# A transformer layer with pooling, neighbourhood attention and routed experts: five reorderings ahead of the main loop

## The chip, the cores and the metric

One core of a Trainium2 chip runs the whole layer. The metric is the device time of one execution in microseconds (us), from the first to the last instruction of the program and what lies around it. The engines are PE (TensorE, matmuls), DVE (VectorE), ACT (ScalarE), POOL (GpSimd) and SP (SyncE, whose queue issues most of the DMAs).

## What is computed

The reference, cut to one layer and one batch of 512 tokens with 1,024 columns and 256 context tokens:

```python
mod = silu(c) @ ada_w + ada_b          # six columns of 1,024: shift1, scale1, gate1, shift2, scale2, gate2
hx = modulate(rmsnorm(x, g1n), sh1, sc1);  hc = the same of ctx
zx = hx @ w_in                         # 512 columns each: pool, q, k, v;  context: k, v
pool_x = multiscale_pool(zx_pool, pool_w) * pool_scale      # windows 2, 4, 8, 16
attn_x = neighbourhood_attention(q, k, v, k_ctx, v_ctx, rpb)
x = x + gate1 * (concat(pool_x, attn_x) @ w_out)
h2 = modulate(rmsnorm(x, g2n), sh2, sc2)
# experts: per token 8 heads, top 16 of 128 + 128 keys, top 16 of the sums -> 128 of 16,384 experts
x = x + gate2 * sum_k softmax(score)_k * gelu(h2 . u_k) * v_k
out = rmsnorm(x, final_g)
```

## The kernel before, in words

The work stands in one program of some 22,000 instructions, in stages.

**Start and `w_in`.** The tokens are turned and normalised, the first two modulation columns are made, and then eight groups of 256 columns of `w_in` are multiplied (loop of line 344), in the order 4, 5 (keys), 6, 7 (values), 2, 3 (queries), 0, 1 (pooling). Every product is made as three matmuls of a high and a low half of each operand (`mm3`, line 66); the halves of a weight block come from `load_split` (line 82): a 1 MB load into one of three `raw` buffers, a copy on ScalarE (`whi`, lines 72 and 550) and a subtraction on VectorE (`wlo`, lines 73 and 556), each with two buffers. `ada_more` (line 320) makes the later modulation columns: four 1 MB loads through the same three `raw` buffers and eight multiply-adds of 1,024 columns on VectorE (line 130). Columns 2, 3, 4 stand in this loop, column 5 (the second gate) in the attention.

**Attention.** 32 steps, four token blocks by eight heads (loop of line 511). `scores` (line 437) is two or three matmuls, one VectorE reduction (line 453) and an exponential on ScalarE; `turn` (line 458) transposes on TensorE; `values` (line 466) multiplies. A turn follows its score by two steps, values by one more. Into these steps `pooling` of the four groups is put (line 392: three to six VectorE adds, one matmul, then a copy and a subtraction into `mixh` and `mixl`), the last gate at step 17, and six of the sixteen units of the out-projection (`out_unit`, line 492: 24 matmuls for 128 tokens by 256 columns). The other ten come behind.

**Norm2.** `norm_T` (line 186) squares each of the four token tiles, makes a diagonal of the root, and for each of eight column blocks turns and scales the four tiles on TensorE (line 195), modulates on ScalarE (line 199), and splits on VectorE (lines 201 and 202). `keepD` turns one of the tiles back (line 572).

**Routing.** Eight blocks of query weights give 16 query products; `topk_unit` (line 632) scores one token tile on four keys sets and takes the top 16 on VectorE. `decode` (line 696) turns them into experts for three tiles, on VectorE. Then 24 batches build the dense weights W (`wbatch_dve`, `wbatch_pe`), which go to memory in twelve writes. Beside all of it run the first 52 of 128 products of the expert matrix `u` with the tokens (`ahead_unit`, line 644: 24 matmuls, a Gelu, every second one a write to memory and a split of the next pair). `pace` (line 844) puts them in: each decode part has a cost in us of VectorE, written out by hand (4.3, 2.9, 0.3, 6.5, 3.2, 4.2 for a tile), the cost divided by `UNIT_DVE` is added to a credit, each W batch adds `UNIT_W`, and a whole credit issues a product.

**Main loop.** For each of the 128 blocks of 128 experts: a product with `u` if it was not made ahead (line 982), a multiplication by W (line 1005), and 18 matmuls with `v` (line 1026). The fourth token tile goes another way, by 256 gathers on POOL with one VectorE operation each (lines 889 and 895).

**Order.** From the end of the first `w_in` group to the end of norm2 the framework orders each engine's instructions itself: by the order in the program as priority, by when it thinks operands and buffers are ready, and by its own durations. From `wq_unit` on, the order on each engine is the one written. Each engine runs its own queue in order; so does SyncE with the loads that it issues.

Of the kernel before, what the change touches and what calls it, by code (L numbers as in the profile page):

```python
# [16 lines left out]
P = 128  # L17
D = 1024
# [9 lines left out]
NAHEAD = 52  # L28
UNIT_DVE = 3.02
UNIT_W = 1.02  # L30
GF, GA = 2, 1
GX = 5
N5 = 17
# [19 lines left out]
def _build(tc, nc, es, A, out, taps):  # L53
# [131 lines left out]

    def norm_T(tiles, a_of, b_of, hi, lo, runs, pool, pst, keep=None):
        n = len(tiles)
        dg = pool.tile([P, 4, P], F32, tag="pr", name="dg", bufs=3)
        for t, x in enumerate(tiles):
            r = rstd_of(x, pool)  # L190
            nc.vector.tensor_scalar(dg[:, t, :], identf, r, None, op0=OP.mult)
        for k in range(KC):
            pt = pst.tile([P, 512], F32, tag="T", name="pT")
            for t in range(n):
                nc.tensor.matmul(pt[:, t * P:(t + 1) * P], tiles[t][:, k * P:(k + 1) * P], dg[:, t, :],
                                 start=True, stop=True)
            tmp = pool.tile([P, 512], F32, tag="pr", name="htmp", bufs=3)
            for dst, src in runs:
                act(dst(tmp), src(pt), AF.Identity, bias=b_of(k), scale=a_of(k))
            w = n * P  # L200
            nc.vector.tensor_copy(hi[:, k, :w], tmp[:, :w])
            nc.vector.tensor_sub(lo[:, k, :w], tmp[:, :w], hi[:, k, :w].bitcast(F32))
            if keep is not None:
                keep(k, tmp)
# [115 lines left out]
    def ada_more(c):  # L320
        acc = ada_dve(c, fp, "m8", 2)
# [16 lines left out]

    def order_kj(g):
        if g == 4:  # L340
            return [(k, j) for k in range(KC) for j in range(2)]
        return [(k, j) for j in range(2) for k in range(KC)]

    for g in (4, 5, 6, 7, 2, 3, 0, 1):
        whi, wlo = {4: w_first, 5: w_next}.get(g) or load_split(A["w_in"][g])
        if g in (3, 0, 1):
            ada_more({3: 2, 0: 3, 1: 4}[g])
        sec, half = divmod(g, 2)
        if sec == 3:
            for t in range(6):  # L350
                pt = psf.tile([P, 512], F32, tag="S", name="pz")
                sh, sl = (hhi, hlo) if t < 4 else (chi, clo)
                c0 = (t if t < 4 else t - 4) * P
                for k in range(KC):
                    mm3(pt[:, :256], sh[:, k, c0:c0 + P], sl[:, k, c0:c0 + P], whi[:, k, :], wlo[:, k, :],
                        k == 0, k == KC - 1)
                act(VN[t][:, half * 256:half * 256 + 256], pt[:, :256], AF.Copy)
            continue
        pzs = [psf.tile([P, 512], F32, tag="S", name="pz") for _ in range(2)]
        for k, j in order_kj(g):  # L360
            cs = slice(j * P, (j + 1) * P)
            mm3(pzs[j], whi[:, k, cs], wlo[:, k, cs], hhi[:, k, :], hlo[:, k, :], k == 0, k == KC - 1)
        if g == 4:
            start.close()
        for j in range(2):
            jj = half * 2 + j
            cs = slice(j * P, (j + 1) * P)
            pt = pzs[j]
            if sec == 2:
                act(KT[jj][:, :SEQ], pt, AF.Copy)  # L370
                pc = psf.tile([P, 512], F32, tag="O", name="pz2")
                for k in range(KC):
                    mm3(pc[:, :CTX], whi[:, k, cs], wlo[:, k, cs], chi[:, k, :], clo[:, k, :], k == 0, k == KC - 1)
                act(KT[jj][:, SEQ:], pc[:, :CTX], AF.Copy)
            elif sec == 1:
                for e in range(2):
                    r = slice(e * 64, e * 64 + 64)
                    act(QZ[jj][r, e, 0:384], pt[r, 64:448], AF.Copy, scale=-0.125)
                    act(QZ[jj][r, e, 384:512].rearrange("p (a c) -> p a c", c=64), edges(pt[r, :]), AF.Copy, scale=-0.125)
            else:  # L380
                xp = fp.tile([P, 528], F32, tag="xp", name="xp", bufs=4)
                nc.vector.memset(xp[:, 0:8], 0.0)
                nc.vector.memset(xp[:, 520:528], 0.0)
                act(xp[:, 8:520].rearrange("p (r c) -> p r c", c=64), pt.rearrange("p (c r) -> p r c", r=8), AF.Copy)
                xps.append(xp)

    mixh = persist.tile([P, KC, SEQ], F32R, tag="hhi", name="mixh")
    mixl = persist.tile([P, KC, SEQ], F32R, tag="hlo", name="mixl")

    def pooling(g, x):
# [44 lines left out]
    def scores(b, h):  # L437
# [18 lines left out]
        return b, h, pr, kb  # L456

# [112 lines left out]
    def keepD(k, tmp):  # L570
        pt = psf.tile([P, 512], F32, tag="O", name="pD")
# [3 lines left out]
    norm_T(xq, lambda k: a2[:, k:k + 1], lambda k: modT[:, 24 + k, 0:1], hhi, hlo,  # L575
           [(lambda t: t, lambda p: p)], fp, psf, keepD)
# [86 lines left out]
    for u in range(20):  # L663
# [586 lines left out]
```

## Time and profile before

| what | value |
|---|---|
| median of 3 runs | 1554.18 us (1554.18 to 1554.66) |
| profiled execution | 1554.02 us, its span 1552.2 us |
| PE busy | 1504.5 us, 97% of the span |
| DVE busy | 1208.3 us, 78% |
| ACT busy | 614.0 us, 40% |
| POOL busy | 348.7 us, 22% |
| mean granted clock of TensorE | 0.991 |
| DMA | 396.67 MB, mean 256 GB/s |

Busy time is the time in which an engine runs an instruction; matmuls are pipelined and their ends are modelled, so a TensorE busy all the time is not one at its peak. A granted clock of 1.00 stands for 2.4 GHz and 0.50 for 1.2 GHz; a mean between them over a stretch tells how much of it was at half.

### The profile page before, as it was taken

Reading aid. Unit: us, or ns where it says so; the run is one execution under the profiler, and the core shown is the slowest. Engines: PE = TensorE matmul, PEld = TensorE weight load, DVE = VectorE, ACT = ScalarE, POOL = GpSimd, SP = SyncE. Lnnn points to the kernel's source line nnn. Section 1 sums busy time; section 2 is a strip of 40 time slices with the busy share of each in tenths; the row PEclk is TensorE's granted clock in tenths of the full one; section 3 lists DMA queues with packets and bytes.
Section 4 is the critical chain, followed back from the end, with each engine's and each line's share of the span. In section 5 each row is a group of like instructions: output and inputs, shape, how many; then the busy total and the mean of one; then the engine's idle time right before and its main releaser. Section 6 shows DMA issues by size and latency. Waiting matters only on the chain.

```text
span 1552.2 us, 22062 instructions
## 1 busy us (share of the span) xinstructions
PE 1504.5 (97%) x8553; PEld 1348.8 (87%) x8553; DVE 1208.3 (78%) x2211; ACT 614.0 (40%) x884; POOL 348.7 (22%) x278
## 2 busy tenths in 40 slices
PE   7999999999989999998999999999999999999997
PEld 4897789888979999997889898889988988899886
DVE  6618853538989999867887888779788887887885
ACT  3522553423334455554333433333333333343343
POOL 0000000000000000000244444344444444445431
PEclk9999999999999999999999999999999999999999
DMA  9318610132235467687799999999899989898971
GB/s 363 132 55 305 241 55 1 55 119 92 99 117 183 178 255 300 247 304 263 250 354 366 349 361 338 346 341 370 311 376 351 361 319 350 319 393 315 373 258 55
DMA packets 135589, 396.67 MB, mean 256 GB/s; under 512 B 9270, under 2 KB 62134, under 8 KB 120252
## 3 DMA queue, kind: packets, MB, share of 16 engines
q1 hardware_dynamic: 91992, 224.32, 40.1%
q0 software_dynamic: 36864, 134.23, 23.4%
q10 hardware_dynamic: 6628, 36.71, 6.0%
q8 instruction: 67, 1.10, 0.3%
q14 instruction: 38, 0.31, 0.1%
HBM read 357.73 MB, written 37.49 MB: 255 GB/s over the span
## 4 chain that ended last, share of the span: by engine, by line
PE 68%; DVE 2%; issue 0%; ACT 0%; POOL 0%; POOLq 0%; DVEq 0%; ACTq 0%
PE acc L67 11%; PE acc L68 11%; PE acc L69 11%; PE pa L67 11%; PE pa L69 11%; PE pa L68 11%; PE wp L823 3%; DVE wlo L556 0%; DVE y L1043 0%; DVE y L1042 0%; DVE gm L809 0%; ACT whi L550 0%; ACT y L1063 0%; DVE pos L623 0%; DVE cand L626 0%
## 5 line engine op out<-in xcount | busy, mean ns | idle before, releaser
L69 PE MATMUL pa<-h2hi,wlo 128*128 128x384 f32 (+1 forms) x1152 | 396.7, 344 | 7.5 <-DVE wlo L556 7.5
L67 PE MATMUL pa<-h2hi,whi 128*128 128x384 f32 (+1 forms) x1152 | 400.0, 347 | 0.0
L68 PE MATMUL pa<-h2lo,whi 128*128 128x384 f32 (+1 forms) x1152 | 396.3, 344 | 0.0
L67 PE MATMUL acc<-vh,wah 128*128 128x512 f32 x768 | 300.5, 391 | 6.4 <-issue 5.0
L68 PE MATMUL acc<-vl,wah 128*128 128x512 f32 x768 | 300.8, 392 | 0.0
L69 PE MATMUL acc<-vh,wal 128*128 128x512 f32 x768 | 299.8, 390 | 0.0
L882 POOL DMA_INDIRECT gr<-in_u,eD x128 | 162.1, 1266 | 512.1 <-ACT wah L1007 303.4
L69 PEld LDWEIGHTS pa<-h2hi,wlo 128*128 128x128 f32 x1152 | 217.3, 189 | 14.5 <-DVE wlo L556 8.7
L67 PEld LDWEIGHTS pa<-h2hi,whi 128*128 128x128 f32 x1152 | 217.5, 189 | 8.1
L68 PEld LDWEIGHTS pa<-h2lo,whi 128*128 128x128 f32 x1152 | 217.5, 189 | 8.0
L882 POOL DMA_INDIRECT gr<-in_v,eD x128 | 174.4, 1362 | 209.3 <-DVE accD L895 177.2
L895 DVE SCALAR_TENSOR_TENSOR accD<-gr,dots,accD 128x1024 f32<-128x1024 f32 x128 | 164.3, 1284 | 32.1 <-DMA gr<-in_v,eD 30.4
L889 DVE SCALAR_TENSOR_TENSOR gr<-gr,h2D 128x1024 f32<-128x1024 f32 x128 | 154.0, 1222 | 37.8 <-DMA gr<-in_u,eD 37.5
L556 DVE TENSOR_TENSOR wlo<-raw,whi 128x2048 fp32r<-128x2048 f32 x59 | 134.9, 2287 | 52.9 <-ACT whi L550 52.9
L67 PEld LDWEIGHTS acc<-vh,wah 128*128 128x128 f32 x768 | 144.8, 189 | 35.2 <-issue 5.3
L69 PEld LDWEIGHTS acc<-vh,wal 128*128 128x128 f32 x768 | 144.7, 188 | 31.0 <-DVE wal L1014 0.5
L68 PEld LDWEIGHTS acc<-vl,wah 128*128 128x128 f32 x768 | 144.8, 189 | 28.0 <-DVE vl L996 0.5
L550 ACT ACTIVATE whi<-raw 128x2048 fp32r<-128x2048 f32 x59 | 112.6, 1909 | 21.8 <-PE po L69 11.0
L989 ACT ACTIVATE vh<-raw 128x1024 fp32r<-128x1024 f32 x74 | 78.5, 1060 | 107.7 <-PE acc L69 107.7
L984 ACT ACTIVATE a<-pa 128x384 f32<-128x384 f32 x76 | 37.4, 492 | 171.9 <-PE pa L69 171.8
L996 DVE TENSOR_TENSOR vl<-raw,vh 128x1024 fp32r<-128x1024 f32 x74 | 90.3, 1220 | 4.4 <-ACT vh L989 4.3
L1007 ACT ACTIVATE wah<-a 128x384 fp32r<-128x384 f32 x76 | 39.9, 525 | 116.1 <-DVE a L1005 116.1
(253 smaller groups left out, 2067.2 us busy)
## 6 DMA issues: line engine op xcount, KB each, us to landing
raw<-in_u SPq DMA_DIRECT2D x51, 1024.0 KB, 5.5
raw<-in_v SPq DMA_DIRECT2D x37, 1024.0 KB, 7.6
vraw<-in_v SPq DMA_DIRECT2D x27, 1024.0 KB, 7.9
w_dram<-stg ACTq DMA_DIRECT2D x12, 2048.0 KB, 7.4
wt<-w_dram SPq DMA_DIRECT2D x32, 768.0 KB, 13.9
awr<-in_ada SPq DMA_DIRECT2D x16, 1024.0 KB, 4.9
vraw<-in_u SPq DMA_DIRECT2D x13, 1024.0 KB, 9.5
a_dram<-apair ACTq DMA_DIRECT2D x26, 384.0 KB, 4.2
```

Of the source, the lines that this page charges most:

```text
L67: nc.tensor.matmul(o, lh, rh, start=start, stop=False)
L68: nc.tensor.matmul(o, lh, rl, start=False, stop=False)
L69: nc.tensor.matmul(o, ll, rh, start=False, stop=stop)
L550: act(hi, raws[n], AF.Copy)
L556: nc.vector.tensor_sub(lo, raws.pop(n), parts[n][0].bitcast(F32))
L823: nc.tensor.matmul(wp[:, x, :], flat(ohj, 4 * q + x), flat(G[m], 4 * q + x), start=m == 0, stop=m == 1)
L882: nc.gpsimd.indirect_dma_start(out=r, out_offset=None, in_=A[kind], in_offset=bass.IndirectOffsetOnAxis(ap=ED[:, s:s + 1], axis=0))
L889: nc.vector.scalar_tensor_tensor(r, r, 1.0, h2D, op0=OP.mult, op1=OP.mult, accum_out=dots[:, s:s + 1])
L895: nc.vector.scalar_tensor_tensor(accD, r, wD[:, s:s + 1], accD, op0=OP.mult, op1=OP.add)
L989: act(vh, vrs[seq[x]], AF.Copy)
L996: nc.vector.tensor_sub(vl, vrs.pop(i), vs[i][0].bitcast(F32))
L1007: act(wah, avals[i], AF.Copy)
```

## The change

Five things. (a) The `w_in` groups run in the order 4, 5, 6, 7, 0, 1, 2, 3; `pooling` of a group stands right behind its columns, its results are kept in one tile of four groups, and one copy and one subtraction put all of them into `mixh` and `mixl`. The modulation columns 2, 3, 4, 5 stand at groups 6, 7, 1, 3, their sums in the buffers of the context tokens. (b) In the last `w_in` group the bias loads and the first two scores stand between its two halves. (c) Nine units of the out-projection instead of six stand inside the attention, and the third weight pair gets buffers of its own. (d) Norm2 squares 768 and 256 columns apart, turns the first three tiles for six column blocks, then the fourth tile. (e) 56 products are made ahead instead of 52, `UNIT_DVE` is 2.85 instead of 3.02, `UNIT_W` 1.05 instead of 1.02, the credit starts at 0 instead of 0.4, `pace` stops two products short, and these two stand behind the last W batch. The last top-k unit stands ahead of two products instead of behind them.

The diff, cut to its core:

```diff
-NAHEAD = 52
-UNIT_DVE = 3.02
-UNIT_W = 1.02
+NAHEAD = 56
+UNIT_DVE = 2.85
+UNIT_W = 1.05
+HOLD = 2
...
-    def load_split(src, t=None):
+    def load_split(src, t=None, pool=None):
         t = t or load_raw(src)
-        hi = stream.tile([P, KC, 256], F32R, tag="whi", name="whi", bufs=2)
-        lo = stream.tile([P, KC, 256], F32R, tag="wlo", name="wlo", bufs=2)
+        hi = (pool or stream).tile([P, KC, 256], F32R, tag="m8" if pool else "whi", name="whi", bufs=2)
+        lo = (pool or stream).tile([P, KC, 256], F32R, tag="m8" if pool else "wlo", name="wlo", bufs=2)
         split(t, hi, lo)
...
     def ada_more(c):
-        acc = ada_dve(c, fp, "m8", 2)
+        acc = ada_dve(c, fp, "cx", 2)
...
+    ADA_AT = {6: 2, 7: 3, 1: 4, 3: 5}
...
-    for g in (4, 5, 6, 7, 2, 3, 0, 1):
-        if g in (3, 0, 1):
-            ada_more({3: 2, 0: 3, 1: 4}[g])
...
         pt = ps1.tile([P, 512], F32, tag="p1", name="pp")
         nc.tensor.matmul(pt, pw, po, start=True, stop=True)
-        ps_ = fp.tile([P, 512], F32, tag="pool", name="psd", bufs=3)
-        act(ps_, pt, AF.Copy, scale=psc[:, g:g + 1])
-        nc.vector.tensor_copy(mixh[:, g, :], ps_)
-        nc.vector.tensor_sub(mixl[:, g, :], ps_, mixh[:, g, :].bitcast(F32))
+        if not pooled:
+            pooled.append(fp.tile([P, 4, 512], F32, tag="m8", name="psd", bufs=2))
+        act(pooled[0][:, g, :], pt, AF.Copy, scale=psc[:, g:g + 1])
...
+    def early_scores():
+        for n in range(H):
+            ld_bias(n)
+        for n in range(2):
+            q1.append(scores(*steps[n]))
+
+    for g in (4, 5, 6, 7, 0, 1, 2, 3):
+        whi, wlo = {4: w_first, 5: w_next}.get(g) or load_split(A["w_in"][g])
+        if g in ADA_AT:
+            ada_more(ADA_AT[g])
...
+        pzs = [psf.tile([P, 512], F32, tag="T" if g == 3 and j else "S", name="pz") for j in range(2)]
+        for k, j in order_kj(g):
+            cs = slice(j * P, (j + 1) * P)
+            if g == 3 and j == 1 and k == 0:
+                to_qz(2, pzs[0])
+                early_scores()
+            mm3(pzs[j], whi[:, k, cs], wlo[:, k, cs], hhi[:, k, :], hlo[:, k, :], k == 0, k == KC - 1)
...
+                xps.append(xp)
+                pooling(jj, xp)
...
+    act(mixh[:, 0:4, :], pooled[0], AF.Copy)
+    nc.vector.tensor_sub(mixl[:, 0:4, :], pooled[0], mixh[:, 0:4, :].bitcast(F32))
...
-            wout[g] = load_split(A["w_out"][g])
+            wout[g] = load_split(A["w_out"][g], pool=fp if g == 2 else None)
...
-    units = {20: (0, 0), 23: (0, 1), 26: (1, 0), 29: (1, 1), 31: (0, 2), 33: (1, 2)}
+    units = {15: (0, 0), 19: (1, 0), 22: (0, 1), 25: (2, 0), 28: (1, 1), 31: (0, 2), 33: (2, 1), 34: (1, 2), 35: (2, 2)}
     for n in range(NS4 + 5):
-        if n in (2, 6, 10, 14):
-            pooling((n - 2) // 4, xps[(n - 2) // 4])
-        if n == N5:
-            ada_more(5)
         if n < NS4:
-            q1.append(scores(*steps[n]))
+            if n >= 2:
+                q1.append(scores(*steps[n]))
...
+    def scale2(t):
+        st = fp.tile([P, 4], F32, tag="st2", name="st2", bufs=4)
+        scr = fp.tile([P, D], BF, tag="pool", name="sq2", bufs=3)
+        act(scr[:, :768], xq[t][:, :768], AF.Square, accum_out=st[:, 0:1])
+        act(scr[:, 768:], xq[t][:, 768:], AF.Square, accum_out=st[:, 1:2])
+        nc.vector.tensor_scalar(st[:, 2:3], st[:, 0:1], 1.0 / D, EPS, op0=OP.mult, op1=OP.add)
+        nc.vector.scalar_tensor_tensor(st[:, 2:3], st[:, 1:2], 1.0 / D, st[:, 2:3], op0=OP.mult, op1=OP.add)
+        nc.gpsimd.tensor_tensor(st[:, 3:4], st[:, 2:3], mhalf[:, 0:1], op=OP.pow)
+        nc.vector.tensor_scalar(dg2[:, t, :], identf, st[:, 3:4], None, op0=OP.mult)
...
+    for k in range(6):
+        pts2[k] = psf.tile([P, 512], F32, tag="TSO"[k % 3], name="pT")
+        turn2(k, (0, 1, 2))
+    for k in range(KC):
+        if k < 6:
+            turn2(k, (3,))
+        else:
+            pts2[k] = psf.tile([P, 512], F32, tag="TSO"[k % 3], name="pT")
+            turn2(k, range(4))
+        ready2(k)
...
+        if u >= 4:
+            topk_unit((u - 4) // 4, TBS[(u - 4) % 4])
         if u == 19:
             ahead_unit()
             ahead_unit()
-        if u >= 4:
-            topk_unit((u - 4) // 4, TBS[(u - 4) % 4])
...
-    credit = [0.4]
+    credit = [0.0]
...
-        while credit[0] >= 1 and state["ahead"] < NAHEAD:
+        while credit[0] >= 1 and state["ahead"] < NAHEAD - HOLD:
```

`turn2(k, ts)` is the turning matmul of column block k for the tiles ts, and `ready2(k)` modulates and splits the block and turns one tile back, as `norm_T` and `keepD` did.

## Rows read from the trace of the kernel before

**Rows 1.** Waits of PE, the two longest: us in total, times, longest.
```profile
PE pa L69 <- DVE wlo L556: 7.5, 4, 6.0
PE acc L67 <- issue: 5.0, 1, 5.0
```

**Rows 2.** Busy us by stage: PE, PEld, DVE, ACT, POOL, PEclk, DMA share, GB/s.
```profile
45.00:160.00 115.00, 115.00 (x685) 100.66 (x685) 64.33 (x80) 40.43 (x71) 0.00 (x0) 0.99 0.44 165
160.00:206.00 46.00, 42.38 (x266) 35.23 (x265) 40.26 (x82) 25.85 (x53) 0.00 (x0) 1.00 0.53 190
...
262.00:294.50 32.50, 30.29 (x259) 29.95 (x258) 17.09 (x29) 9.74 (x10) 1.21 (x2) 1.00 0.18 66
294.50:314.50 20.00, 16.52 (x99) 14.57 (x98) 12.26 (x24) 10.88 (x21) 1.40 (x3) 0.91 0.12 42
...
428.00:470.00 42.00, 34.74 (x188) 33.78 (x187) 34.47 (x158) 14.95 (x16) 0.81 (x1) 0.92 0.39 139
...
538.00:547.00 9.00, 5.95 (x46) 5.61 (x45) 8.97 (x9) 4.60 (x6) 0.00 (x0) 0.81 0.42 160
...
690.00:715.00 25.00, 19.73 (x90) 17.27 (x90) 11.12 (x44) 10.08 (x13) 0.00 (x0) 0.86 0.89 325
715.00:1540.00 825.00, 823.63 (x4031) 732.86 (x4030) 683.95 (x893) 301.70 (x383) 337.67 (x259) 1.00 0.90 326
```

**Rows 3.** Timeline around norm2: start, us, engine, line, operation [idle before].
```profile
295.75 1.16 PE L195 MATMUL pT<-dg,xq 128*128 128x128 f32 x8 [0.81 <-DVE dg L191]
298.94 0.71 PE L195 MATMUL pT<-dg,xq 128*128 128x128 f32 x4 [2.03 <-DVE dg L191]
...
300.28 0.43 DVE L201 CAST h2hi<-htmp 128x512 fp32r<-128x512 f32 x1 [1.39 <-ACT htmp L199]
300.74 0.69 DVE L202 TENSOR_TENSOR h2lo<-htmp,h2hi 128x512 fp32r<-128x512 f32 x1
...
302.06 0.78 ACT L199 ACTIVATE htmp<-pT,modT,a 128x512 f32<-128x512 f32 x1 [0.20 <-PE pT L195]
...
314.41 0.60 ACT L617 ACTIVATE pqT<-pa 128x512 f32<-128x512 f32 x1 [4.52 <-PE pa L69]
```

**Rows 4.** Groups of DVE, 160 to 206 us: count, busy us, mean ns.
```profile
L130 DVE SCALAR_TENSOR_TENSOR aacc<-awr,cc,aacc 128x1024 f32<-128x1024 f32 x8 | 10.2, 1281 | 0.0
L453 DVE CUSTOM_DVE_ANT_1 pr<-ps,bias 128x512 f32<-128x512 f32 x15 | 10.2, 686 | 1.1 <-PE ps L447 0.8 <-PE tp L461 0.2
```

**Rows 5.** Timeline of the last top-k unit and the first decode.
```profile
434.07 2.27 DVE L556 TENSOR_TENSOR wlo<-raw,whi 128x2048 fp32r<-128x2048 f32 x1
441.20 0.87 DVE L621 MAX8 sv<-sc 128x8 f32<-128x128 f32 x4 [4.86 <-ACT sc L639]
...
446.07 0.99 DVE L701 TENSOR_TENSOR cand<-sv 128x128 f32<-128x128 f32 x8
...
451.01 2.29 DVE L556 TENSOR_TENSOR wlo<-raw,whi 128x2048 fp32r<-128x2048 f32 x1
...
462.14 2.29 DVE L556 TENSOR_TENSOR wlo<-raw,whi 128x2048 fp32r<-128x2048 f32 x1
...
433.66 0.49 ACT L655 ACTIVATE apair<-pa 128x384 f32<-128x384 f32 x1 [2.56 <-PE pa L69]
437.82 0.49 ACT L655 ACTIVATE apair<-pa 128x384 f32<-128x384 f32 x1 [3.67 <-PE pa L69]
...
438.77 1.92 ACT L550 ACTIVATE whi<-raw 128x2048 fp32r<-128x2048 f32 x1 [0.46 <-ACT apair L655]
```

**Rows 6.** Timeline of the hand-over to the main loop.
```profile
698.35 0.38 SPq L964 DMA_DIRECT2D wt<-w_dram  x1
...
706.52 1.06 ACT L989 ACTIVATE vh<-vraw 128x1024 fp32r<-128x1024 f32 x1 [7.58 <-DMA vraw<-in_v]
...
708.09 0.76 PE L67 MATMUL acc<-vh,wah 128*128 128x512 f32 x1 [5.03 <-issue]
```

**Rows 7.** DMA issues of the modulation chunks: count, KB each, us to landing.
```profile
awr<-in_ada SPq DMA_DIRECT2D x16, 1024.0 KB, 4.9
```

More of the change, by code (lines that the diff above doesn't have):

```diff
@@ L184, in rstd_of @@
         return st[:, 0:1]
[L186 to L204, printed above, removed]
     def edges(t):
@@ L342, in order_kj @@
         return [(k, j) for j in range(2) for k in range(KC)]
-    for g in (4, 5, 6, 7, 2, 3, 0, 1):
-        whi, wlo = {4: w_first, 5: w_next}.get(g) or load_split(A["w_in"][g])
-        if g in (3, 0, 1):
-            ada_more({3: 2, 0: 3, 1: 4}[g])
[L348 to L385, printed above, removed]
@@ L387, in _build @@
-    mixh = persist.tile([P, KC, SEQ], F32R, tag="hhi", name="mixh")
-    mixl = persist.tile([P, KC, SEQ], F32R, tag="hlo", name="mixl")
+    pooled = []
     def pooling(g, x):
@@ L456, in scores, with to_qz @@
         return b, h, pr, kb
+    q1 = []
+    def to_qz(jj, pt):
+        for e in range(2):
+            r = slice(e * 64, e * 64 + 64)
+            act(QZ[jj][r, e, 0:384], pt[r, 64:448], AF.Copy, scale=-0.125)
+            act(QZ[jj][r, e, 384:512].rearrange("p (a c) -> p a c", c=64), edges(pt[r, :]), AF.Copy, scale=-0.125)
+    def early_scores():
[7 more added lines that the diff above has]
+            ada_more(ADA_AT[g])
+        sec, half = divmod(g, 2)
+        if sec == 3:
+            for t in range(6):
+                pt = psf.tile([P, 512], F32, tag="S", name="pz")
+                sh, sl = (hhi, hlo) if t < 4 else (chi, clo)
+                c0 = (t if t < 4 else t - 4) * P
+                for k in range(KC):
+                    mm3(pt[:, :256], sh[:, k, c0:c0 + P], sl[:, k, c0:c0 + P], whi[:, k, :], wlo[:, k, :],
+                        k == 0, k == KC - 1)
+                act(VN[t][:, half * 256:half * 256 + 256], pt[:, :256], AF.Copy)
+            continue
+        pzs = [psf.tile([P, 512], F32, tag="T" if g == 3 and j else "S", name="pz") for j in range(2)]
[5 more added lines that the diff above has]
+            mm3(pzs[j], whi[:, k, cs], wlo[:, k, cs], hhi[:, k, :], hlo[:, k, :], k == 0, k == KC - 1)
+        if g == 4:
+            start.close()
+        for j in range(2):
+            jj = half * 2 + j
+            cs = slice(j * P, (j + 1) * P)
+            pt = pzs[j]
+            if sec == 2:
+                act(KT[jj][:, :SEQ], pt, AF.Copy)
+                pc = psf.tile([P, 512], F32, tag="O", name="pz2")
+                for k in range(KC):
+                    mm3(pc[:, :CTX], whi[:, k, cs], wlo[:, k, cs], chi[:, k, :], clo[:, k, :], k == 0, k == KC - 1)
+                act(KT[jj][:, SEQ:], pc[:, :CTX], AF.Copy)
+            elif sec == 1:
+                if jj != 2:
+                    to_qz(jj, pt)
+            else:
+                xp = fp.tile([P, 528], F32, tag="xp", name="xp", bufs=4)
+                nc.vector.memset(xp[:, 0:8], 0.0)
+                nc.vector.memset(xp[:, 520:528], 0.0)
+                act(xp[:, 8:520].rearrange("p (r c) -> p r c", c=64), pt.rearrange("p (c r) -> p r c", r=8), AF.Copy)
+                xps.append(xp)
+                pooling(jj, xp)
@@ L458, in turn @@
+    mixh = persist.tile([P, KC, SEQ], F32R, tag="hhi", name="mixh")
+    mixl = persist.tile([P, KC, SEQ], F32R, tag="hlo", name="mixl")
+    act(mixh[:, 0:4, :], pooled[0], AF.Copy)
+    nc.vector.tensor_sub(mixl[:, 0:4, :], pooled[0], mixh[:, 0:4, :].bitcast(F32))
     def turn(b, h, pr, kb):
@@ L504, in out_unit @@
         nc.vector.tensor_add(xq[t][:, cs], xq[t][:, cs], tmp)
-    for n in range(H):
-        ld_bias(n)
-    q1, q2, q3 = [], [], []
-    units = {20: (0, 0), 23: (0, 1), 26: (1, 0), 29: (1, 1), 31: (0, 2), 33: (1, 2)}
+    q2, q3 = [], []
+    units = {15: (0, 0), 19: (1, 0), 22: (0, 1), 25: (2, 0), 28: (1, 1), 31: (0, 2), 33: (2, 1), 34: (1, 2), 35: (2, 2)}
     NS4 = len(steps)
     for n in range(NS4 + 5):
-        if n in (2, 6, 10, 14):
-            pooling((n - 2) // 4, xps[(n - 2) // 4])
-        if n == N5:
-            ada_more(5)
         if n < NS4:
-            q1.append(scores(*steps[n]))
+            if n >= 2:
+                q1.append(scores(*steps[n]))
             if n >= 2 * H:
@@ L568, in _build, with turn2, ready2 @@
     h2D = persist.tile([P, D], F32, tag="row", name="h2D")
-    def keepD(k, tmp):
-        pt = psf.tile([P, 512], F32, tag="O", name="pD")
+    dg2 = fp.tile([P, 4, P], F32, tag="pr", name="dg2", bufs=3)
+    def scale2(t):
[7 more added lines that the diff above has]
+        nc.vector.tensor_scalar(dg2[:, t, :], identf, st[:, 3:4], None, op0=OP.mult)
+    def turn2(k, ts):
+        for t in ts:
+            nc.tensor.matmul(pts2[k][:, t * P:(t + 1) * P], xq[t][:, k * P:(k + 1) * P], dg2[:, t, :],
+                             start=True, stop=True)
+    def ready2(k):
+        tmp = fp.tile([P, 512], F32, tag="pr", name="htmp", bufs=3)
+        act(tmp, pts2[k], AF.Identity, bias=modT[:, 24 + k, 0:1], scale=a2[:, k:k + 1])
+        nc.vector.tensor_copy(hhi[:, k, :], tmp)
+        nc.vector.tensor_sub(hlo[:, k, :], tmp, hhi[:, k, :].bitcast(F32))
+        pt = ps1.tile([P, 512], F32, tag="p1", name="pD")
         nc.tensor.transpose(pt[:, 0:P], tmp[:, 384:512], identf)
         act(h2D[:, k * P:(k + 1) * P], pt[:, 0:P], AF.Copy)
-    norm_T(xq, lambda k: a2[:, k:k + 1], lambda k: modT[:, 24 + k, 0:1], hhi, hlo,
-           [(lambda t: t, lambda p: p)], fp, psf, keepD)
+    for t in range(4):
+        scale2(t)
+    pts2 = {}
+    for k in range(6):
+        pts2[k] = psf.tile([P, 512], F32, tag="TSO"[k % 3], name="pT")
+        turn2(k, (0, 1, 2))
+    for k in range(KC):
+        if k < 6:
+            turn2(k, (3,))
+        else:
+            pts2[k] = psf.tile([P, 512], F32, tag="TSO"[k % 3], name="pT")
+            turn2(k, range(4))
+        ready2(k)
     tap("h2D", h2D)
```

1 line of the change is left out of this document (removed).

## The prediction

> **What bounds the kernel now.** I read, in this order, the waits of TensorE, the busy time by stage, and the timelines of the stages that do not fill TensorE. From 45 to 160 us and in the main loop, from 715 to 1540 us, TensorE is busy all the time, at a granted clock of 0.99 to 1.00 (of 2.4 GHz); the reader is to see there that nothing but fewer matmuls could shorten these stretches [rows 2]. The change keeps every matmul: it reorders. So all that it can win is the time in which TensorE waits or runs at half clock (1.2 GHz). The waits name the worst places: a weight half `wlo` that VectorE has not made yet, and one wait of 5.0 us before the first `acc` product [rows 1].
>
> By stage, idle time is the window less TensorE's busy time [rows 2]. **Attention and out-projection**: 46.00 - 42.38 + 32.50 - 30.29 = 5.8 us. **Decode**: 42.00 - 34.74 = 7.3 us and, at the first W batch, 9.00 - 5.95 = 3.1 us. **Hand-over** to the main loop: 25.00 - 19.73 = 5.3 us. A mean clock of 0.92 over 42 us is 6.7 us at half speed, which takes 3.4 us if no wait lies in it; part of it does, I count 2.4 us. In the same way 0.81 over 9 us takes 1.7 us, and 0.86 over 25 us 3.5 us, of which I count 3.0. So decode loses 7.3 + 3.1 + 2.4 + 1.7 = 14.5 us and the hand-over 8.3 us. **Norm2** is read as a chain: the last out-projection product ends at 294.5 us, where that window ends, and the first query product of the next stage is evicted at 314.4 us: 19.9 us [rows 2, 3].
>
> **Attention (groups reordered, early scores, nine out-projection units inside).** VectorE is busy 40.26 of the 46 us from 160 to 206 us [rows 2]. Of that 10.2 us are the last gate's multiply-adds and 10.2 us the scores' own reductions [rows 4]; the rest is mostly pooling and weight splits. The change moves gate and pooling into the 45 to 160 us stage. At most 40.3 - 10.2 = 30.1 us move there, where VectorE is busy 64.33 of 115 us; 94 of 115 fits, so I cost the move at nothing, and that idle half is its cover. Loads move with it: the gate's four 1 MB chunks go past `w_in` and `w_out` loads on SyncE's queue, through the same three buffers. The 2.2 us of idle time at the end, from 262 us on, lay where a weight pair was split while only one unit was left to cover it; now the third pair has buffers of its own, and nine units fill the drain. What is late next: the pooled groups' copy and subtraction, each 2,048 wide, so some 1.9 and 2.3 us [rows 5], stand on ScalarE and VectorE just as attention starts, covered by two finished scores and two more on TensorE. I leave 1.8 of the 5.8 us standing and count **4.0 us**; the ends are 0 (other joints just as late) and 5.8.
>
> **Norm2 by tile.** Before, the last tile's diagonal arrives 298.94 - 294.5 = 4.4 us after the last out-projection product [rows 3]. The new chain squares 256 columns after that product instead of 1,024 and has one short VectorE operation more; I take the same 4.4 us as its bound. Over it TensorE turns tiles 0 to 2 for six column blocks: 18 products, of which four last at most 1.16 us [rows 3], so 0.24 to 0.29 us each, 4.3 us. That wait is gone to 0.1 us. What sets the end next is VectorE: copy 0.43 and subtraction 0.69 us for each of eight blocks, 9.0 us [rows 3]. From the last out-projection product: 4.3 + 0.24 (tile 3) + 0.78 (first modulation on ScalarE) + 9.0 + 0.7 (the three products on the last block, 4.16 / 24 x 512 / 384 each [rows 5]) = 15.0, with 0.5 for the joints 15.5 us, against 19.9: **4.4 us**. Ends: 1.0 (turns and evictions as interleaved as before) and 6 us.
>
> Rows decide on the clock here: waits of 3.6 us in all from 160 to 206 us left it at 1.00, the two waits of 2.8 us around 297 us took it to 0.91 over 20 us [rows 2, 3]. I count no fall in the new norm2, whose waits are short. The Trainium skill, "TensorE: Matmul & The Clock Gate", section "A second HAM failure mode: psum-queue depth-cycling", says that short idle moments between groups of matmuls are enough to send the clock back and forth, which speaks against this change. By that rule two more falls would make the total some 3.4 us longer than my sum.
>
> **Decode: the last top-k unit ahead of two products, and more products per decode time.** That unit takes 441.20 to 446.07 us, 4.9 us, on VectorE, after 4.86 us of idle time in which TensorE made the two products; the unit before it ended at 434.07 us, where the split stands [rows 5]. Moved ahead it runs from there: the idle time goes, and decode starts 5.1 us earlier. But the split for product 6 (counted from 0) now stands behind it: ready at 434.1 + 4.9 + 2.3 = 441.3 us. TensorE ends number 5 at 437.7 us (its eviction starts at 437.82), does the two parts of number 6 that do not need that half (0.3 us) and waits 3.3 us. Products take 4.16 us (433.66 to 437.82) [rows 5]: 6 to 9 end at 441.3 + 3.8 + 12.5 = 457.6 us. VectorE: candidates and first top-8, 4.9 us (446.07 to 451.01), a split, 8.8 us up to the next one (453.3 to 462.14), a split: 441.3 + 4.9 + 2.3 + 8.8 + 2.3 = 459.6 us [rows 5]; number 10 waits 1.7 us. If the first wait halves the clock for a while, that falls into this second wait. From there 21.4 / 2.85 = 7.5 products a tile take 31 us of TensorE, and 21.4 + 3.75 x 2.3 = 30 us of VectorE: TensorE sets the pace. At the first W batch VectorE comes 5.1 us earlier, less 2 to 3 us of new waits for ScalarE's halves; TensorE comes 4.2 (one product more) - 2.3 (7.3 against 5.0 us of waits) - 2.4 (clock) = 0.5 us earlier. So the 3.1 us there become 0.5 to 1.5; I take 1.5. Together 3.3 + 1.7 + 1.5 = 6.5, with 1.0 for joints 7.5, against 14.5: **7.0 us**. Ends: 2 (each wait only moved) and 12.
>
> **Hand-over: two products kept.** The first `acc` product runs at 708.1 us after a wait from 703.1 us, and before that stand three products, from some 690.3 us, where the last W product ends. In those 18 us lie the write of the last W block, the load of `wt` at 698.35 us on SyncE's queue, behind it `vraw`, and its split at 706.52 us [rows 6]. By the planner's own costs (64.2 / 2.85 + 25 x 1.05 = 48.8, against 54 - 6 = 48 wanted) one paced product comes at the last call, after the W products, and the two kept ones follow: six products, 25 us, over those 18. The wait and the fall of the clock go. SyncE gets one raw load ahead of `wt` that waits for a split, some 1 us, covered by the 7 us left over. **8.3 us**; ends 5.0 and 8.5.
>
> **Main loop.** Four products, 16.6 us, move from a stage that TensorE fills into one that it almost fills, and two more pairs go to memory and back: nothing won or lost by itself. VectorE is busy 684 of 825 us, so 679 of 808 after; the DMA share of 0.90 becomes 0.91 [rows 2]. I count 0; ends 0 and a loss of 17.
>
> **Sum.** 4.0 + 4.4 + 7.0 + 8.3 = 23.7 us. The profiled execution took 1554.0 us, 1.8 us of it outside its span, and is 0.2 us under the median of the runs: 1554.0 - 23.7 = **1530.3 us**.
>
> **Rivals.** (1) The framework orders the front by its own idea of durations, and what it saves in attention and norm2 it loses at other joints: front gain 0, 1538.7 us. For it: attention's idle time arose under the same ordering. Against: TensorE has no idle time from 45 to 160 us. Chance 0.16. (2) Decode's waits only move: 1537.3 us; for it two of three waits are left in my own walk. 0.10. (3) The clock falls twice more, 1.7 us each: 1533.7 us, 0.05. (4) The main loop is bound by transfers or VectorE and does not shorten: 1547 us; for it the DMA share of 0.90, against it that TensorE idles 1.4 of 825 us. 0.04. (5) **Slower**: the `w_in` stage starves. The chunks of gates 2 and 3 now stand between `w_in` loads in the three shared buffers, each holding one for 4.9 us of landing [rows 7] and two multiply-adds, 2.6 us [rows 4]. A group takes 115 / 8 = 14.4 us and a load is asked for about two groups ahead, 28.8 us. Through two buffers four chunks take 15 us; with 4.9 + 1.9 + 2.3 us for load and split behind them, 24, they are in time. Through one buffer it is 39 us, 10 us late. From one free buffer on this decides; at two groups it is 20 us, and with no other gain in front 1538.7 + 20 = 1559 us. 0.05. That the change does not do what it says would be a kept product that slips ahead of the last W product; the others still cover the 18 us but for 1 to 5 us, inside the range. The forecast keeps 0.60.
>
> **Numbers.** The range takes the ends together: gains of 11 to 32 us, 1522 to 1543 us; outside lie rivals 4 and 5 and the tails, some 0.13. A measurement of this kernel can tell 0.2%, 3.1 us, from no change. Only rival 5 and a little of 1 and 4 give no gain: faster 0.92, same 0.02, slower 0.06.
>
> **What would show it.** In the waits of TensorE: no `acc` wait of 5 us, and a clock of 1.00 around the hand-over; `pa` waiting for `wlo` some 5 us in two waits, 3.3 of them before product 6; the first `pqT` 15 to 16 us after the last out-projection product; VectorE busy under 30 of the first 46 us of attention. Wrong would be a wait of TensorE between 45 and 160 us, new idle time in the main loop, or a decode in which TensorE idles over 10 us.

## The result and the profile after

The changed kernel takes **1534.06 us** (median of 4 runs, 1533.04 to 1536.22) against 1554.18 us beside it: 20.1 us less, ratio 0.9872 [0.9855, 0.9889]. Forecast were 1530.3 us, range 1522 to 1543. The profiled execution is the longest of the four: 1536.22 us, span 1534.5 us.

The waits of TensorE in the changed kernel (us in total, times, longest) answer to [rows 1]:

```profile
PE pa L69 <- DVE wlo L553: 3.7, 4, 3.0
PE pD L591 <- ACT htmp L587: 2.3, 5, 0.5
PE wp L853 <- DVE gm L839: 1.5, 3, 0.9
PE acc L67 <- ACT wah L1037: 1.4, 1, 1.4
```

Here `pa` is a product with `u` or with query weights, `pD` a block turned back, `htmp` a modulated block, `wp` the products of a W batch, `gm` their operand from VectorE, and `acc` and `wah` are the sums and an operand of the main loop. The wait of 5.0 us before the first `acc` is gone, `wlo` is waited for half as long, and a wait is new: `pD` for `htmp`, in norm2. [rows 1] shows the two longest waits behind the start; one wait of 9.6 us in the start, ahead of everything that was reordered, is longer (8.8 us in the changed kernel).

Busy time by stage, the columns as in [rows 2]; the bounds are moved to the same places of the changed kernel:

```profile
45.00:160.00 115.00, 114.78 (x670) 97.76 (x669) 82.76 (x115) 39.03 (x63) 0.00 (x0) 0.96 0.59 217
160.00:206.00 46.00, 44.76 (x279) 38.63 (x278) 22.45 (x41) 29.94 (x62) 0.00 (x0) 1.00 0.20 69
262.00:292.30 30.30, 29.52 (x251) 29.38 (x250) 15.11 (x32) 8.89 (x17) 1.65 (x3) 1.00 0.11 36
292.30:312.40 20.10, 17.81 (x99) 14.76 (x98) 11.85 (x22) 9.44 (x19) 0.85 (x2) 0.83 0.20 63
427.00:470.00 43.00, 40.01 (x221) 39.18 (x220) 40.68 (x170) 17.07 (x18) 0.81 (x1) 0.96 0.49 168
...
684.00:710.00 26.00, 25.80 (x149) 25.39 (x148) 8.68 (x8) 10.08 (x14) 0.00 (x0) 1.00 0.89 336
710.00:1525.00 815.00, 813.07 (x3959) 720.48 (x3957) 684.22 (x929) 297.12 (x384) 333.56 (x260) 1.00 0.91 331
```

The hand-over (684 to 710 us) is full at a clock of 1.00, where it had 0.86. In attention VectorE is busy 22.45 of 46 us instead of 40.26, and its work stands in the 45 to 160 us stage. Norm2 (fourth line) still has 2.3 us of idle time, and its clock is lower: 0.83 against 0.91. The clock of the `w_in` stage is lower too, 0.96 against 0.99.

The table gives the length of the stages in us, read from the timelines, for every kernel that was run (the experiments follow). "Front" is from the first `w_in` product to the last out-projection product, "norm2" from there to the first `pqT`, "routing" from the last `pqT` to the last W product, with the products made by then in brackets, "hand-over" from there to the first `acc`, "main" the rest. Query products take 93.6 us in all of them. The start, ahead of the first `w_in` product, is left out; it took 43.7 to 47.2 us and differs between executions, so differences of these stages and of whole runs agree only within some 2 us.

| kernel | front | norm2 | routing | hand-over | main |
|---|---|---|---|---|---|
| before | 249.5 | 19.9 | 282.0 (52) | 18.1 | 844.1 |
| after | 248.3 | 20.1 | 278.0 (53) | 25.4 | 825.0 |
| late_only | 250.6 | 19.7 | 278.1 (53) | 25.4 | 824.2 |
| hold_only | 250.4 | 19.6 | 282.9 (52) | 29.5 | 824.3 |
| front_only | 247.0 | 19.3 | 281.9 (52) | 18.0 | 844.0 |
| topk_only | 252.0 | 20.9 | 275.2 (52) | 18.0 | 844.1 |
| norm2_old | 246.4 | 20.1 | 278.1 (53) | 25.4 | 823.9 |
| norm2_free | 246.5 | 14.0 | 278.1 (53) | 25.4 | 823.9 |
| decode_mend | 248.1 | 20.2 | 277.1 (54) | 22.6 | 824.9 |
| both_mends | 246.7 | 14.0 | 277.1 (54) | 23.1 | 824.9 |
| after_again | 248.2 | 20.1 | 278.1 (53) | 25.4 | 824.0 |
| decode_held | 247.0 | 19.3 | 273.0 (53) | 25.4 | 824.5 |
| mends_held | 247.2 | 14.0 | 273.0 (53) | 25.4 | 824.0 |

Before against after: routing is 4.0 us shorter and makes a product (4.17 us) more, 8.1 us. Hand-over and main together are 862.2 against 850.4 us; without that product the gain is 11.8 - 4.2 = 7.6 us. The front gains 1.2 us, norm2 nothing in these two profiles. Norm2 has to be read beside its clock: the new order took 19.3 us where the stage's mean clock was 0.91 (front_only, decode_held) and 20.1 to 20.2 us where it was 0.83 (after, after_again, decode_mend); the old order took 19.6 to 20.1 us at 0.91 and 20.9 us at 0.84 (topk_only). At a like clock the new order is thus 0.3 to 0.8 us shorter.

### The profile page after: what moved, and what is told of

Read it like the earlier page. It is cut to its first block, busy times and chain, and to the rows that moved or that the text cites. A ratio compares the mean times of both kernels' runs of the same rounds, so it can differ in the third digit from the quotient of the medians.

```text
span 1534.5 us, 22100 instructions
## 1 busy us (share of the span) xinstructions
PE 1502.8 (98%) x8553; PEld 1347.2 (88%) x8553; DVE 1203.8 (78%) x2208; ACT 612.2 (40%) x893; POOL 343.3 (22%) x278
## 3 DMA queue, kind: packets, MB, share of 16 engines
q0 software_dynamic: 36864, 134.23, 23.7%
## 4 chain that ended last, share of the span: by engine, by line
PE 53%; issue 8%; POOL 4%; DVE 3%; DMA 3%; ACT 1%; POOLq 0%; ACTq 0%; DVEq 0%
PE pa L69 9%; PE pa L67 9%; PE pa L68 9%; PE acc L67 8%; PE acc L68 8%; PE acc L69 8%; POOL gr L912 4%; DMA gr<-in_v,eD 3%; PE wp L853 3%; DVE wlo L553 1%; DVE gr L919 0%; ACT whi L547 0%; DVE gm L839 0%; DVE y L1073 0%; DVE y L1072 0%
## 5 line engine op out<-in xcount | busy, mean ns | idle before, releaser
L912 POOL DMA_INDIRECT gr<-in_u,eD x128 | 158.7, 1240 | 520.4 <-ACT wah L1037 310.7
```

Source lines behind the costliest of these rows:

```text
L912: nc.gpsimd.indirect_dma_start(out=r, out_offset=None, in_=A[kind], in_offset=bass.IndirectOffsetOnAxis(ap=ED[:, s:s + 1], axis=0))
```

## The experiments

The kernels were timed beside the kernel before: the first four of the table on one chip, the next four on a second, the last three on a third. The kernel before took 1553.6, 1553.8 and 1554.3 us on them.

| kernel | median us (lowest to highest) | ratio to before |
|---|---|---|
| late_only | 1537.58 (1537.01 to 1538.35) | 0.9897 [0.9882, 0.9912] |
| hold_only | 1544.93 (1543.85 to 1545.98) | 0.9944 [0.9930, 0.9957] |
| front_only | 1550.88 (1550.31 to 1554.50) | 0.9983 [0.9974, 0.9992] |
| norm2_old | 1534.06 (1533.79 to 1536.47) | 0.9879 [0.9864, 0.9894] |
| topk_only | 1549.70 (1546.40 to 1552.50) | 0.9969 [0.9958, 0.9980] |
| norm2_free | 1529.99 (1528.24 to 1531.88) | 0.9845 [0.9830, 0.9859] |
| decode_mend | 1533.50 (1532.07 to 1537.45) | 0.9876 [0.9858, 0.9893] |
| both_mends | 1526.82 (1525.17 to 1531.16) | 0.9828 [0.9812, 0.9845] |
| after_again | 1537.39 (1535.54 to 1538.46) | 0.9886 [0.9871, 0.9902] |
| decode_held | 1530.95 (1528.70 to 1532.96) | 0.9847 [0.9832, 0.9861] |
| mends_held | 1525.18 (1523.59 to 1526.70) | 0.9812 [0.9798, 0.9825] |

### The parts one by one

**late_only**: the kernel before with part (e) alone.

```diff
-NAHEAD = 52
-UNIT_DVE = 3.02
-UNIT_W = 1.02
+NAHEAD = 56
+UNIT_DVE = 2.85
+UNIT_W = 1.05
+HOLD = 2
...
-    credit = [0.4]
+    credit = [0.0]
```

The top-k unit ahead of the two products and the stop two short of `NAHEAD` are taken with it.

> The kernel before with part (e) alone (56 products ahead, two kept, new rates, the top-k unit moved). Theory A, the terms of the prediction hold: decode 7.0 and hand-over 8.3 us, 15.3 us faster, about 1539 us. Theory B, read from the two traces: decode and W stage gave 8.2 us and the hand-over 8.2 us, 16 to 17 us faster, about 1537.5 us. Rival C, the late gains need the front's new timing: less than 10 us.

**front_only**: the changed kernel with this part undone, so parts (a) to (d) alone.

> The changed kernel with part (e) undone. Theory A: attention 4.0 and norm2 4.4 us, 8.4 us faster than before, about 1546 us. Theory B: norm2 gives nothing and attention 1 to 5 us, by how often the clock falls in front: 1549 to 1553 us.

**hold_only**: the kernel before, whose pace stops at 52 as it did, with four more products behind the last W batch.

```diff
-NAHEAD = 52
+NAHEAD = 56
+HOLD = 4
```

> The kernel before with the pace unchanged up to 52 products, and four more kept behind the last W product. Theory A and B alike: only the 5.0 us wait and the half clock at the hand-over go, 8.3 us faster, about 1546 us, decode's waits as before. Rival C, the wait only moves to the next load of the main loop: under 3 us faster.

**topk_only**: the kernel before with the order of the last top-k unit alone.

```diff
+        if u >= 4:
+            topk_unit((u - 4) // 4, TBS[(u - 4) % 4])
         if u == 19:
             ahead_unit()
             ahead_unit()
-        if u >= 4:
-            topk_unit((u - 4) // 4, TBS[(u - 4) % 4])
```

> The kernel before with one edit: the last top-k unit stands ahead of the two products instead of behind them; rates, credit, 52 products and the end of the pace as before. Theory A (the move does it: VectorE's 4.86 us of idle time go and the new wait of some 3 us lies beside VectorE's work): 5 to 6 us faster than before, some 1548; the wait of 5 us before the first acc stays. Theory B (the waits only move, and what decode gained in the change comes from the new rates): 0 to 2 us faster, some 1552 to 1554, with new waits for wlo that add up to the 7.5 us of before.

late_only wins 16.1 us and front_only 2.8, together 18.9 of the 20.1 us: the gain lies nearly all in part (e). hold_only wins 8.7 us. The waits of TensorE show the difference, first in hold_only:

```profile
PE pa L70 <- DVE wlo L557: 8.2, 4, 6.0
PE wp L824 <- DVE gm L810: 3.0, 2, 2.1
```

then in front_only:

```profile
PE pa L68 <- DVE wlo L552: 7.7, 4, 6.0
PE acc L66 <- issue: 4.9, 1, 4.9
PE wp L852 <- DVE gm L838: 3.0, 2, 2.1
PE pD L590 <- ACT htmp L586: 2.5, 5, 0.5
```

and in topk_only:

```profile
PE acc L67 <- issue: 5.0, 1, 5.0
PE pa L69 <- DVE wlo L556: 3.2, 2, 3.0
PE wp L823 <- DVE gm L809: 3.0, 2, 2.1
```

Products behind the last W batch take away the `acc` wait and nothing else; the order of the unit halves the `wlo` wait and nothing else; parts (a) to (d) leave both. In topk_only the routing is 282.0 - 275.2 = 6.8 us shorter with the same 52 products, so of the 8.1 us the order of one unit gives 6.8 and the rest of part (e), its rates above all, about 1.3; the `wp` wait falls by about as much, from 3.0 to 1.5 us. By the medians its runs win 4.1 us (95% interval 3.1 to 6.5), below that and below the 5 to 6 expected: its profiled front and norm2 are 3.5 us longer than before, with a mean clock of 0.96 from 160 to 206 us and of 0.84 in norm2, and its runs are 6 us apart.

One thing in the hand-over is not what the change says. With `HOLD = 0` the program comes out the same, instruction by instruction: the credit reaches 54 at the last call anyway. It is 56 products with these rates that keep two of them, not the stop.

### Norm2

**norm2_old**: the changed kernel with the old `norm_T` and `keepD` in the place of the new norm2.

> The changed kernel with norm2 as it was (four tiles squared and turned block by block). Theory A, the new norm2 is worth 4.4 us: 1538 us or more. Theory B, it is worth nothing, since its turned-back blocks hold the product queue and the clock falls: within 1.5 us of the changed kernel, 1533 to 1535.5 us, and the chain from the last out-projection product to the first query eviction about 20 us in both.

Its time is that of the changed kernel, and its norm2 stage is as long, 20.1 us. The timeline of norm2 in the changed kernel (start, us, engine, line, operation) shows what has become of the gain:

```profile
292.15 5.30 PE L582 MATMUL pT<-dg,xq 128*128 128x128 f32 x46
...
300.55 0.33 PE L591 MATMUL pD<-small,htmp 128*128 128x128 f32 x1 [0.42 <-ACT htmp L587]
...
303.89 0.47 PE L591 MATMUL pD<-small,htmp 128*128 128x128 f32 x1 [0.36 <-ACT htmp L587]
304.06 0.80 PE L67 MATMUL pa<-h2hi,whi 128*128 128x512 f32 x1
...
297.41 0.43 DVE L588 CAST h2hi<-htmp 128x512 fp32r<-128x512 f32 x1 [1.60 <-ACT htmp L587]
297.87 0.69 DVE L589 TENSOR_TENSOR h2lo<-htmp,h2hi 128x512 fp32r<-128x512 f32 x1
...
305.08 0.69 DVE L589 TENSOR_TENSOR h2lo<-htmp,h2hi 128x512 fp32r<-128x512 f32 x1
...
312.43 0.60 ACT L647 ACTIVATE pqT<-pa 128x512 f32<-128x512 f32 x1 [7.75 <-PE pa L69]
```

The wait for the diagonal is gone: TensorE turns from 292.15 us on without a stop. The first split block is ready at 298.56 us, but the first product that needs it, `pa`, starts at 304.06, behind the last of the eight turned-back blocks `pD`. Each `pD` needs a modulated block, and ScalarE makes these one at a time, with the copies of `pD` in between. So the splits end at 305.08 + 0.69 = 305.77 us, and the eviction `pqT` comes 6.7 us later.

**norm2_free** takes the turned-back blocks out of that place:

```diff
+    hts = [fp.tile([P, 4, 512], F32, tag="m8", name="htmp", bufs=2) for _ in range(2)]
...
-        tmp = fp.tile([P, 512], F32, tag="pr", name="htmp", bufs=3)
+        tmp = hts[k // 4][:, k % 4, :]
...
-        pt = ps1.tile([P, 512], F32, tag="p1", name="pD")
-        nc.tensor.transpose(pt[:, 0:P], tmp[:, 384:512], identf)
+
+    def back2(k):
+        pt = psf.tile([P, 512], F32, tag="TSO"[k % 3], name="pD")
+        nc.tensor.transpose(pt[:, 0:P], hts[k // 4][:, k % 4, 384:512], identf)
...
+    for k in range(KC):
+        back2(k)
```

> The changed kernel, but the modulated blocks of norm2 stay in two free buffers of four and are turned back only behind the eighth block, through other PSUM buffers, so that the first products need not wait for the turned-back blocks. Theory A (these eight blocks, which stand ahead of the products in TensorE's queue and in their two PSUM buffers, took away what the diagonals' wait gave): the first pa stands at about the end of the first split instead of 5.5 us behind it, last out-projection product to first pqT is 15.5 to 16.5 us instead of 20.1, and the run is 3 to 5 us faster than the changed kernel, some 1530. Theory B (the splits on VectorE, 9 us, or the clock set that end anyway): at most 1 us faster, and the first products then wait for h2lo one by one.

Its timeline of norm2, and below it the window of the stage as in [rows 2]:

```profile
293.08 7.33 PE L582 MATMUL pT<-dg,xq 128*128 128x128 f32 x64
300.37 0.44 PE L595 MATMUL pD<-small,htmp 128*128 128x128 f32 x2
300.56 0.48 PE L67 MATMUL pa<-h2hi,whi 128*128 128x512 f32 x1
...
305.49 0.69 DVE L591 TENSOR_TENSOR h2lo<-htmp,h2hi 128x512 fp32r<-128x512 f32 x1
...
297.53 5.47 ACT L589 ACTIVATE htmp<-pT,modT,a 128x512 f32<-128x512 f32 x8 [1.93 <-PE pT L582]
...
307.27 0.60 ACT L653 ACTIVATE pqT<-pa 128x512 f32<-128x512 f32 x1 [2.93 <-PE pa L69]
```

```profile
292.50:312.50 20.00, 20.00 (x127) 17.32 (x126) 11.75 (x23) 9.72 (x20) 1.09 (x3) 1.00 0.19 61
```

ScalarE makes eight blocks without a break, `pa` starts with the splits, and `pqT` comes 1.1 us behind the last split (306.18). TensorE is busy 20.00 of 20 us at a clock of 1.00; the stage is 14.0 instead of 20.1 us, and the run 4.1 us shorter by the medians, on another chip. The edit changes buffers and order together, so which of the two held `pa` back was not tried apart. In norm2_old, whose `pD` go through other buffers than the products, the first `pa` (305.34 us) stands behind the turns and seven `pD` too, 6.9 us behind the first split: a place in the queue is enough for such a wait.

### Decode

**decode_mend**: the split for product 6 (and the load behind it) ahead of the last top-k unit instead of in `ahead_unit`, and one product more behind the first candidates.

```diff
-            sp_lo(8 + n + 1)
-            ld(8 + n + 4)
+            if parts[8 + n + 1][1] is None:
+                sp_lo(8 + n + 1)
+                ld(8 + n + 4)
...
+        if u == 19:
+            sp_lo(11)
+            ld(14)
...
+        if t == 0:
+            yield UNIT_DVE
```

> The changed kernel with two edits in decode: the split of the weight half for product 6 stands ahead of the last top-k unit, and one product more is paced, behind the candidates of the first tile. Theory A (the two waits left there, 3.0 and some 1 us, and the fall of the clock at 438.9 are all that decode still loses, and the pace has a product too few at this place): both waits under 0.5 us, no half clock from 430 to 470 us, 5 to 6 us faster than the changed kernel, some 1528. Theory B (VectorE sets decode's end, so the waits only move to the first W batches): wp waits longer by what pa waits less, 0 to 2 us faster, some 1532 to 1534.

**both_mends** is norm2_free with this.

> The two kernels norm2_free and decode_mend together. If the two places are independent (theory A of both): the sum of the two gains over the changed kernel within 1 us, 8 to 11 us faster, some 1523 to 1526. If VectorE, which is given work of norm2 and of decode in one order, passes one gain on into a wait of the other (theory B): less than two thirds of the sum.

In both, the decode waits are gone and the clock is 1.00 from 428 to 470 us. But TensorE's waits in decode_mend show where a part went:

```profile
PE wp L859 <- DVE gm L845: 1.3, 2, 0.9
PE acc L67 <- issue: 1.2, 1, 1.2
```

The product added in decode is one less behind the last W batch: 22.6 us stand there, the transfers need that long, and the `acc` wait is back. decode_mend's runs win only 0.6 us, against the 5 to 6 expected and 3.7 us in its stages (routing 0.9 and hand-over 2.8). both_mends is 7.2 us faster than the changed kernel, short of the 8 to 11 expected, and 3.2 us faster than norm2_free, as much as its routing and hand-over give (0.9 and 2.3), though its profiled main loop is 1.0 us longer. Since decode_mend and the changed kernel were timed on different chips, the changed kernel ran again as **after_again**, and beside it **decode_held** and **mends_held**, which are decode_mend and both_mends with one product less paced among the W batches:

```diff
-UNIT_W = 1.05
+UNIT_W = 1.01
```

> The changed kernel itself, on the chip of the two runs beside it, since the kernels compared so far were timed on different chips. Theory A (its runs differ by how often the clock falls in the front, up to the end of norm2, and those falls differ from one execution to the next): some 1534, runs 2 to 4 us apart, the longer ones at the lower mean clock. Theory B (the chip makes the difference): another median than 1534.1 by over 1.5 us, with runs that agree within 1 us.

> decode_mend with UNIT_W 1.01 instead of 1.05: one product goes from the W batches behind the last W product, so that six products and not five cover the 21 to 22 us up to the first acc. Theory A (decode_mend gave 3.7 us between the last query product and the first acc, 5 in decode less the new wait of 1.2 us at the hand-over, and its runs as a whole were as long as the changed kernel's because of falls of the clock in the front): no acc wait behind issue, last pqT to first acc 298 to 299 us (303.4 in the changed kernel, 299.7 in decode_mend), and 4 to 5 us faster than after_again on this chip. Theory B (mending decode moves its waits to later stages): within 2 us of after_again.

> both_mends with UNIT_W 1.01 instead of 1.05: the same one product is kept for the hand-over. Theory A: the wait of 1.7 us before the first acc is gone, 1 to 1.7 us faster than both_mends, some 1525, and 9 to 10 us faster than after_again on this chip. Theory B (VectorE, busy 121 of 130 us among the W batches, sets the length of that stage once a product less fills it): wp waits for gm by 1 to 2 us more there, and the time stays at 1526 to 1527.

The windows of decode, from 425 us on, and of the hand-over, from 676 us on, in mends_held:

```profile
425.00:468.00 43.00, 43.00 (x250) 43.00 (x249) 41.34 (x186) 17.89 (x19) 0.81 (x1) 1.00 0.48 171
...
676.00:704.00 28.00, 27.80 (x155) 26.75 (x154) 14.41 (x58) 12.38 (x14) 0.00 (x0) 1.00 0.93 332
```

TensorE is busy throughout, the `acc` wait is gone, and no product is lost: the routing takes 273.0 us with 53 products against 278.1. On this chip decode_held is 6.4 us faster than after_again and mends_held 12.2 us, more than was expected for either: by stages the mends give 5.1 us in the routing and, in mends_held, 6.1 in norm2 (5.3 against decode_held, whose clock there was higher). The front is 1.0 to 1.2 us shorter as well, where after_again's clock was low; that is not the mends' doing. The wait of `wp` did not grow (1.3 us). mends_held is the fastest kernel of this study: 1525.18 us, ratio 0.9812 [0.9798, 0.9825] to before.

after_again settled less: half of each theory came true. It took 1537.39 us, not 1534.06, and its runs are 2.9 us apart. The mean clocks of its runs are 0.990 to 0.993; the changed kernel's first four runs have 0.991, 0.995, 0.995 and 0.995, and the one at 0.991 is the long one, which is the profiled one. The profiles of both kernels show the same fall in the front: from 134 to 144 us the granted clock is 0.83 in the changed kernel, and in after_again:

```profile
134.00:144.00 10.00, 9.83 (x43) 0.84 0.56 191
```

The columns are PE busy, clock, DMA share and GB/s. The same window of front_only, which has the same instructions there:

```profile
134.00:144.00 10.00, 9.83 (x49) 1.00 0.50 161
```

So the lengths go with the clock, but why all four runs on that chip were low, while mends_held beside them had 0.994 to 0.997, stays open: chance or chip.

## Why the prediction was right, and where it was not

**Decode** (7.0 us forecast, 8.1 measured): right in mechanism and nearly in size. The idle time of [rows 5] is gone, and the wait before product 6 is there as walked, 3.0 us against 3.3. Here the split of that half, the candidates behind it and the waiting product:

```profile
436.76 2.29 DVE L553 TENSOR_TENSOR wlo<-raw,whi 128x2048 fp32r<-128x2048 f32 x1
438.95 1.00 DVE L731 TENSOR_TENSOR cand<-sv 128x128 f32<-128x128 f32 x8
...
439.11 0.69 PE L69 MATMUL pa<-h2hi,wlo 128*128 128x384 f32 x1 [2.96 <-DVE wlo L553]
```

The second wait, 1.7 us before product 10, did not come; late_only, with 1.4 us there, shows it is a close thing. In its place stands a fall of the clock behind the first wait, which the walk had meant to lie in the second: a mean of 0.96 over 43 us costs some 1.7 us, by the reckoning of the prediction. That the size came out so near is in part luck.

**Hand-over** (8.3 forecast, 7.6 in the profile, 8.7 in hold_only): right in its steps and its size, but not in the margin that it left. Six products cover the transfers, and the three events of [rows 6] now stand so:

```profile
694.05 0.38 SPq L994 DMA_DIRECT2D wt<-w_dram  x1
...
706.13 1.06 ACT L1019 ACTIVATE vh<-vraw 128x1024 fp32r<-128x1024 f32 x1 [0.66 <-DMA vraw<-in_v]
...
709.44 0.39 PE L67 MATMUL acc<-vh,wah 128*128 128x512 f32 x1
```

`vh` is made by 707.2 us, and the products end 2.2 us later: so far reached the cover, and so little was left that decode_mend, a product shorter, waited again. The prediction had 7 us left over, since it took the transfers of before, whose `vh` is made 17.6 us behind the last W product (707.58 - 690.03); now it is 23.1 us (707.19 - 684.07). What lengthened them was not tried. The prediction took the stop for what keeps the products back; the rates do it.

**Attention** (4.0 forecast): idle time fell as counted, from 5.8 us to 1.24 + 0.78 = 2.0 us, and the 45 to 160 us stage took VectorE's work (82.76 of 115 us there) with 0.2 us of idle time. What was off is the clock of that stage, which the term left out. In the profile it is 0.96 instead of 0.99, and the front gains 1.2 us only. Over all profiles, fronts of the old order (before, late_only, hold_only, topk_only) take 250.6 us in the mean, those of the new one 247.3 (nine): 3.3 us. The measured end of front_only as a whole is 2.8 us.

**Norm2** (4.4 forecast, 0 in the profiles, 0.3 to 0.8 at a like clock): the step that failed. VectorE came as forecast: copies begin 5.1 us and splits end 13.5 us behind the last out-projection product, where the walk had 5.3 and 14.3. Wrong was the last summand, 0.7 us for "the three products on the last block". It supposes that the products keep up with the splits. They do not: all 24 of them stand behind eight `pD` in TensorE's queue, which no step of the prediction mentions, though the change moves them into `ps1`, whose two buffers the products use. 6.7 us stand in the place of 0.7. By an estimate, 2.3 of the 6.0 us over are the clock, told of below: from the first `pa` to the first `pqT` it is 312.43 - 304.06 = 8.4 us here and 314.41 - 308.30 = 6.1 us before, where these products ran at a clock of 1.00. The rest is their place in the queue. The trace of before would have shown it: its first `pa` starts at 308.30 us, 6.9 us behind the end of the first split (300.74 + 0.69, [rows 3]).

```profile
308.30 0.47 PE L67 MATMUL pa<-h2hi,whi 128*128 128x512 f32 x1
```

The Trainium skill, "TensorE: Matmul & The Clock Gate", section "Step-by-step: what each phase is for", says that matmuls stay in program order; the trace agrees, `pa` starts right behind the last `pD` with an operand that had been ready for 5.5 us.

The clock was the other part of it. I had counted no fall in norm2; five waits of 0.36 to 0.51 us were followed by a granted clock of 0.50 from 304 to 308 us (columns: PE busy, clock, DMA share, GB/s), the first products of 512 columns take 0.63 us instead of 0.40, and the stage has 0.83.

```profile
304.00:308.00 4.00, 4.00 (x10) 0.50 0.17 23
```

All five profiles with these five waits have such a fall (0.83 or 0.91 over the stage); the three without them, norm2_free, both_mends and mends_held, keep 1.00. The Trainium skill, "TensorE: Matmul & The Clock Gate", section "A second HAM failure mode: psum-queue depth-cycling", which the prediction weighed, says that short idle moments between groups of matmuls send the clock back and forth; these rows agree. Over the whole run rival 3 was not right: what the clock lost in the `w_in` stage and in norm2 it won in decode (0.96 for 0.92) and at the hand-over (1.00 for 0.86), and the mean of both profiles is 0.991.

**Main loop** (0): right; 1.9 us idle of 815. Of the rivals, 1 holds for norm2 alone; 2, 4 and 5 are ruled out by the routing's 8.1 us, the main loop's 844.1 - 825.0 us, and 0.2 us of idle time between 45 and 160 us. The sum by stages, 3.3 + 0 + 8.1 + 7.6 to 8.7 = 19.0 to 20.1 us, against 23.7 forecast and 20.1 measured: the missing norm2 and a little of attention, less what decode gave more. The lower ends of the terms (0, 1.0, 2 and 5.0) add up to 8 us, not to the 11 from which the range was made; the measured gain lies well above both.

## What to carry to other kernels

Taking away the wait at the head of a chain was worth next to nothing here. Look up first who starts next at its end, and what stands in front of that in its engine's queue and in its buffers: eight small transposes, off the path for their results, held the path for their place. Work kept back to cover a transfer is a budget: whoever spends a product of it earlier gets the wait back (decode_mend), and a pace that issues one less in between restores it (decode_held).

## What the runs showed of the hardware

The same instruction stream has a different clock in different executions. From 134 to 144 us the changed front ran at 0.83 and 0.84 (after, decode_mend, after_again) and at 1.00 (the six others with this front, front_only and mends_held among them), with waits of at most 0.2 us there. Before the fall in the changed kernel TensorE made sixteen `pcol` products of one column each; front_only, which kept 1.00, made them too (second line):

```profile
136.73 1.84 PE L136 MATMUL pcol<-ones,aacc 128*128 128x1 f32 x16
...
137.91 1.84 PE L135 MATMUL pcol<-ones,aacc 128*128 128x1 f32 x16
```

So these products alone do not decide it; what does stays open. For a kernel whose edits are worth 1 to 4 us each, such falls are as large as an edit (1533.0 to 1538.5 us over eight runs of one program), so stages were compared, not only whole runs.
